# The opening stage of a hybrid encoder layer: staging of weights, form of the first norm, queue of its stores, and place of two projection tiles

## Chip, core and metric

One core of one Trainium2 chip. The metric is the time of one execution on the device in microseconds; of several runs the median counts. A profiled execution has a time of its own, which is given beside its span.

## What is computed

One encoder layer over 1024 prompt tokens and 64 sample tokens of width 1024. The change touches the first norm, the keys and values of the memory tokens, and the input projection:

```python
hp = _layer_norm(x_prompt, ln_in_g, ln_in_b)        # 1024 tokens
hs = _layer_norm(x_sample, ln_in_g, ln_in_b)        # 64 tokens
mk_p = (mem_prompt @ mem_w_k[l])                    # 256 x 1024, outputs mem_k_p
mv_p = (mem_prompt @ mem_w_v[l])                    # outputs mem_v_p
...
proj = x @ p['w_in']
g_q, g_k, g_v, g_o, g_a, s_u, f_q, f_k, f_v, f_f = jnp.split(proj, offsets, axis=-1)
o_gla, gla_s = _gla_mix(g_q, g_k, g_v, g_o, g_a, ...)
o_s5, s5_re, s5_im = _s5_mix(s_u, ...)

def _layer_norm(x, g, b):
    mu = jnp.mean(xf, axis=-1, keepdims=True)
    var = jnp.mean(jnp.square(xf - mu), axis=-1, keepdims=True)
    y = (xf - mu) * lax.rsqrt(var + LN_EPS) * g + b
```

Behind that come gated linear attention, the S5 state space model, forgetting attention, cross attention into the memory, and a gated ConvFFN. All of it is float32.

## The kernel before

Every matmul is made of three: each operand is split into a high part (`_hi`, `xh`, a rounded float32 that TensorE takes at full rate) and the remainder (`_lo`, `xl`), and `mm3` sums hi x hi, hi x lo and lo x hi. `split_weights` does it for a weight unit of 128 x 1024: SP (SyncE) starts the load into `raw`, ScalarE copies it to `hi`, and GpSimd or VectorE subtracts for `lo`. `raw` has two buffers, `hi` and `lo` have four.

The opening stage loads the memory tokens (`load_mem`, into the buffers of token tiles 6 and 7), transposes them (`mem_features`), and runs four halves of the memory projection (`mem_half`, two for keys and two for values, each over four weight units and two row tiles, out `ps_kv`). Nine token tiles `xr[i]` are loaded (`load_x`; five lie in `xra`, four in `xrb`), and `layer_norm` works on each: VectorE takes statistics (`bn_stats`), GpSimd computes the reciprocal deviation (`rstd_of`, `ln_y`) and the offset `ln_nb`, ScalarE scales in place, VectorE multiplies by `lnw[0]`, GpSimd adds `lnw[1]`. The tile is then stored to `hd` in DRAM from ScalarE's queue and transposed by `to_features` (TensorE into `ps_tr`, ScalarE copies `x0h`, VectorE subtracts `x0l`). Results of `mem_half` go through one buffer, `spare`, and ScalarE's queue to `out_mem_k` and `out_mem_v`. A one-column copy on GpSimd in `load_x` holds a tile's load back until a given weight unit has been split.

Next is the feature projection: `a_tiles` computes tiles of 128 features over all tokens (`ps_a`, two halves of 544 tokens, 96 matmuls of 272 columns for each tile). Tiles 0 and 1 are the S5 input; they are stored to DRAM as `suD` and read back in another layout as U by eight loads. Tiles 2 and 3 are the queries and keys of the linear attention (`gq`, `gk`). `b_proj` computes token-major parts (`ps_b`). The S5 stage runs in four quarters: VectorE computes parameters in a region called `s5r` (R3), GpSimd makes tables from them, TensorE reads U in `s_in` and gives `s_y`. Its parameters come into `p1s`, which lies where `lnw` was.

The program is written in one order, and a scheduler sets each engine's own order from it when the kernel is built, with priorities in the order of writing. At run time each engine and each queue takes its instructions strictly in that order, and a waiting instruction holds back those behind it.

Of the kernel before, what the change touches and what calls it, by code (L numbers as in the profile page):

```python
# [9 lines left out]
F32 = mybir.dt.float32  # L10
# [52 lines left out]
def hybrid_layer(ctx: ExitStack, tc: tile.TileContext, I, O):  # L63
# [45 lines left out]
    G.memset(mhalf, -0.5)  # L109


    def split_weights(src, n, name, eng=None):
        raw = mem.tile([128, 1024], F32, tag="raw", name=name + "_raw", bufs=2)
        hi = mem.tile([128, 1024], F32R, tag="whi", name=name + "_hi", bufs=4)
        lo = mem.tile([128, 1024], F32R, tag="wlo", name=name + "_lo", bufs=4)
        SY.dma_start(out=raw[:, :n], in_=src)
        S.activation(out=hi[:, :n], in_=raw[:, :n], func=AF.Copy)  # L117
        (eng or G).tensor_tensor(out=lo[:, :n], in0=raw[:, :n], in1=hi[:, :n].bitcast(F32), op=SUB)  # L118
        return hi, lo
# [145 lines left out]


    memT = [slot([128, 4, 256], F32R, "memT") for _ in range(4)]
    memx = xr[7], xr[6]
    mem_out = [O[n].rearrange("a b m h d -> (a b m) (h d)") for n in ("mem_k_p", "mem_v_p")]
    wm = []  # L270
    V.memset(xr[8], 0.0)
# [4 lines left out]
    def mem_units(n):  # L276
        for _ in range(n):
            j, u = divmod(len(wm), 4)
            wm.append(split_weights(I[("w_mk", "w_mv")[j // 2]][j % 2, :, 1024 * u:1024 * u + 1024], 1024, "wm",
                                    (V, V, G)[len(wm) % 3]))  # L280

    def mem_features(i):
        both = psd("ps_tr")
# [8 lines left out]
    def mem_half(j):  # L292
        pss = [pse("ps_kv") if j % 2 else pst("ps_kv") for _ in range(2)]
        for k in range(KD):
            w = [u.rearrange("p (k c) -> p k c", k=2)[:, k % 2, :] for u in wm[4 * j + k // 2]]
            for i in range(2):
                mm3(pss[i], [memT[2 * z + k // 4][:, k % 4, 128 * i:128 * i + 128] for z in range(2)], w, k == 0, k == KD - 1)
        for i in range(2):
            S.activation(out=spare, in_=pss[i], func=AF.Copy)
            S.dma_start(out=mem_out[j // 2][128 * i:128 * i + 128, 512 * (j % 2):512 * (j % 2) + 512], in_=spare)  # L300

    def load_x(i, after=None):
        t0, m = token_tile(i)
        if after is not None:
            G.tensor_copy(out=xr[i][:, 0:1], in_=after[0][:, 0:1].bitcast(F32))
        SY.dma_start(out=xr[i][0:m], in_=I["x_prompt"][0, t0:t0 + m, :] if i < 8 else I["x_sample"][0])

    load_mem(0)
    mem_units(2)
    load_mem(1)  # L310
    load_x(0)
    lnw = load_ln(I["ln_in_g"], I["ln_in_b"])
    load_x(1)
    mem_features(0)
    mem_features(1)
    mem_units(2)
    for i, u in zip(range(2, NT), (1, 3, 4, 5, 6, 8, 8)):
        load_x(i, wm[u])
        mem_units(min(2, 16 - len(wm)))
        if i % 2 == 0 and i < 8:  # L320
            mem_half(i // 2 - 1)
    mem_half(3)
    for i in range(NT):
        t0, m = token_tile(i)
        layer_norm(xr[i], lnw)
        S.dma_start(out=hd[128 * i:128 * i + 128, :], in_=xr[i])
        to_features(xr[i], xh, xl, t0, m, True)

    xst = slot([128, KD, 2, 64], F32R, "xst")
    for z in range(2):  # L330
# [357 lines left out]
    go = g5(NT, 256)  # L688
    V.memset(gv[64:128, 8, :], 0.0)
    V.memset(go[64:128, 8, :], 0.0)  # L690
    a_tile(2, plain_evac(gq))
    a_tile(3, plain_evac(gk))
    b_proj(b_weights("w_b1", 280, 3), 280, 3, b1_evac)
    a_tile(4, q_evac(0))
    b_proj(b_weights("w_b2", 256, 4), 256, 4, b2_evac)
# [1006 lines left out]
```

## Time and profile before

| | |
|---|---|
| median of 3 runs | 1766.38 us (1760.13 to 1768.58) |
| time of the profiled execution | 1761.28 us |
| its span, first to last instruction | 1759.6 us |
| TensorE busy in the span | 1658.4 us (94%) |
| mean granted clock of TensorE | 0.976 |

Busy is the time in which an engine had an instruction running. Matmuls overlap, so TensorE's busy time says when it stands still, and the interval between two starts says what a matmul takes. The granted clock is the share of full speed that TensorE was given; 0.5 is the lower of its two levels, 1.2 of 2.4 GHz. A wait is put down to what released the instruction last.

### The profile page before, as it was taken

How to read it: one execution, taken by the hardware profiler on the slowest of the kernel's cores; microseconds unless marked ns; L12 is line 12 of the kernel's file. 1: busy time of each engine (PE TensorE's matmuls, PEld its weight loads, DVE VectorE, ACT ScalarE, POOL GpSimd, SP SyncE). 2: the span in 40 equal slices, each digit the busy share in tenths (PEclk: the TensorE clock that was granted, in tenths of full speed). 3: DMA queues.
4: the chain of work that ended last, by engine and by line, in shares of the span. 5: the costliest groups of instructions: out<-in, count | busy, mean ns of one | idle time of the engine just before them, and what ended most of it. 6: DMA issues, size and time to landing. Idle time of an engine off the chain costs nothing.

```text
span 1759.6 us, 27862 instructions
## 1 busy us (share of the span) xinstructions
PE 1658.4 (94%) x10856; PEld 1457.0 (83%) x10856; DVE 1053.2 (60%) x1802; ACT 694.3 (39%) x1265; POOL 724.9 (41%) x774
## 2 busy tenths in 40 slices
PE   7788999999999999999999899999999999999997
PEld 5588987777767878988777789999999997777775
DVE  6673611665556336124444899877788786785547
ACT  4421224423655235235335654444444445221111
POOL 5765831111001256223223465554555447743322
PEclk9899999999989999999999899999999999999999
DMA  8633232436960410122111212222222227531112
GB/s 287 236 97 59 67 102 75 167 113 183 285 146 25 156 48 24 37 73 72 37 48 68 79 63 76 86 77 81 80 77 75 80 87 259 179 104 44 48 49 101
DMA packets 95754, 178.29 MB, mean 101 GB/s; under 512 B 26207, under 2 KB 48575, under 8 KB 95495
## 3 DMA queue, kind: packets, MB, share of 16 engines
q1 hardware_dynamic: 65462, 136.00, 25.6%
q10 hardware_dynamic: 30160, 40.52, 6.3%
q8 instruction: 85, 1.39, 0.3%
q14 instruction: 47, 0.38, 0.1%
HBM read 129.56 MB, written 46.34 MB: 100 GB/s over the span
## 4 chain that ended last, share of the span: by engine, by line
PE 43%; DVE 7%; issue 4%; POOL 3%; ACT 2%; DMA 2%; POOLq 0%; DVEq 0%; SPq 0%; ACTq 0%
PE ps_d L197 7%; PE u_a L1390 6%; PE u_d L1390 6%; PE u_c L1390 6%; PE ps_a L215 5%; PE ps_o L197 4%; PE u_b L1390 3%; PE m_o L197 1%; PE m_s L197 1%; POOL wd_lo L118 1%; DVE Yb L1556 1%; POOL ln_y L124 1%; DVE Ya L1556 1%; DMA hraw<-hD 1%; POOL ln_y L123 0%
## 5 line engine op out<-in xcount | busy, mean ns | idle before, releaser
L197 PE MATMUL ps_d<-wd_hi,hb 128*128 128x512 f32 x704 | 225.0, 396 | 10.7 <-DVE Ya L1556 3.0
L197 PEld LDWEIGHTS ps_d<-wd_hi,hb 128*128 128x128 f32 x704 | 132.1, 188 | 48.0 <-DVE Yb L1556 3.9
L197 PE MATMUL ps_d<-wd_lo,hb 128*128 128x512 f32 x352 | 139.6, 397 | 1.6 <-POOL wd_lo L118 1.6
L1390 PE MATMUL u_a<-x2A,wu_wlo 128*128 128x288 f32 (+1 forms) x1032 | 139.3, 291 | 0.9 <-DVE x2A L1201 0.9
L1390 PEld LDWEIGHTS u_a<-x2A,wu_wlo 128*128 128x128 f32 x1032 | 134.2, 192 | 1.3 <-DVE x2A L1201 1.3
L1336 POOL TENSOR_TENSOR wu_wlo<-wu_raw,wu_wlo 128x512 fp32r<-128x512 f32 x63 | 97.3, 1547 | 80.7 <-ACT wu_wlo L1335 80.7
L197 PE MATMUL ps_o<-wo_hi,bo 128*128 128x512 f32 x384 | 124.8, 399 | 3.0 <-ACT ps_o L138 2.7
L1463 DVE SCALAR_TENSOR_TENSOR y<-x2B,ffp,y 128x1024 f32<-128x1024 f32 x88 | 124.8, 1419 | 1.1 <-ACT y L1461 1.0
L1493 POOL TENSOR_TENSOR hb<-hraw,hb 128x1024 fp32r<-128x1024 f32 (+1 forms) x40 | 64.9, 1642 | 84.3 <-ACT hb L1492 84.3
L1336 POOL TENSOR_TENSOR wu_whi<-wu_whi 128x512 fp32r<-128x512 f32 x44 | 71.1, 1615 | 61.1 <-ACT wu_whi L1335 60.4
L197 PE MATMUL ps_b<-wb_hi,x0h 128*128 128x512 f32 (+2 forms) x256 | 89.6, 351 | 0.0
L197 PE MATMUL ps_b<-wb_lo,x0h 128*128 128x512 f32 (+2 forms) x256 | 89.2, 348 | 0.0
L197 PE MATMUL ps_b<-wb_hi,x0l 128*128 128x512 f32 (+2 forms) x256 | 89.0, 348 | 0.0
L1335 ACT ACTIVATE wu_wlo<-wu_raw 128x512 fp32r<-128x512 f32 x86 | 54.1, 631 | 88.4 <-DVE wu_raw L1332 34.7
L197 PEld LDWEIGHTS ps_o<-wo_hi,bo 128*128 128x128 f32 x384 | 72.6, 191 | 18.9 <-ACT ps_o L138 3.1
L1556 DVE TENSOR_TENSOR Ya<-Ya,ps_d 128x1024 f32<-128x1024 f32 (+1 forms) x50 | 60.9, 1218 | 44.8 <-PE ps_d L197 39.3
L1018 POOL TENSOR_TENSOR bo<-mixT,bo 128x512 fp32r<-128x512 f32 (+1 forms) x18 | 22.7, 1270 | 150.2 <-ACT bo L1017 150.2
L118 POOL TENSOR_TENSOR wo_lo<-wo_raw,wo_hi 128x1024 fp32r<-128x1024 f32 x14 | 33.2, 2383 | 118.6 <-ACT fx_pt L976 45.6
L197 PEld LDWEIGHTS ps_d<-wd_lo,hb 128*128 128x128 f32 x352 | 66.1, 188 | 17.1 <-POOL wd_lo L118 2.5
L197 PE MATMUL ps_o<-wo_lo,bo 128*128 128x512 f32 x192 | 76.6, 399 | 1.2 <-POOL wo_lo L118 1.2
L118 POOL TENSOR_TENSOR wa_lo<-wa_raw,wa_hi 128x1024 fp32r<-128x1024 f32 x16 | 38.9, 2445 | 93.0 <-ACT wa_hi L117 55.2
L1492 ACT ACTIVATE hb<-hraw 128x1024 fp32r<-128x1024 f32 (+1 forms) x40 | 25.3, 652 | 128.1 <-PE ps_d L197 115.8
(548 smaller groups left out, 4502.0 us busy)
## 6 DMA issues: line engine op xcount, KB each, us to landing
wu_raw<-in_w_up SPq DMA_DIRECT2D x88, 256.0 KB, 2.7
hD<-y ACTq DMA_DIRECT2D x22, 512.0 KB, 2.6
wd_raw<-in_w_dn SPq DMA_DIRECT2D x22, 512.0 KB, 3.5
hraw<-hD SPq DMA_DIRECT2D x20, 544.0 KB, 4.5
fx<-qk SPq DMA_DIRECT2D x28, 256.0 KB, 8.7
fxk<-qk SPq DMA_DIRECT2D x20, 256.0 KB, 4.8
wm_raw<-in_w_mk SPq DMA_DIRECT2D x8, 512.0 KB, 5.8
wm_raw<-in_w_mv SPq DMA_DIRECT2D x8, 512.0 KB, 5.4
```

Source lines behind the costliest of these rows:

```text
L118: (eng or G).tensor_tensor(out=lo[:, :n], in0=raw[:, :n], in1=hi[:, :n].bitcast(F32), op=SUB)
L124: G.tensor_tensor(out=y, in0=y, in1=mhalf[0:v.shape[0], 0:n], op=ALU.pow)
L197: PE.matmul(out, lhsT=lhs[i], rhs=rhs[j], start=start and n == 0, stop=stop and n == 2)
L215: PE.matmul(ps[:, c, 0:272], lhsT=w[i][:, k, :], rhs=xs[j][:, k, t0:t0 + 272], start=k == 0 and n == 0, stop=k == KD - 1 and n == 2)
L1018: G.tensor_tensor(out=sl, in0=part, in1=sh.bitcast(F32), op=SUB)
L1335: S.activation(out=WU[n][0], in_=RAW[n], func=AF.Copy)
L1336: (eng or G).tensor_tensor(out=WU[n][1], in0=RAW[n], in1=WU[n][0].bitcast(F32), op=SUB)
L1390: PE.matmul(ps, lhsT=w[i][:, k, :], rhs=x[j][:, k, c], start=start and k == 0 and q == 0, stop=k == 3 and q == 2, skip_group_check=True)
L1463: V.scalar_tensor_tensor(out=out, in0=u[:, c + j:c + j + n], scalar=cw[j][:, m:m + 1], in1=out, op0=MUL, op1=ADD)
L1492: S.activation(out=t[:, hi:hi + n], in_=r, func=AF.Copy)
L1493: G.tensor_tensor(out=t[:, lo:lo + n], in0=r, in1=t[:, hi:hi + n].bitcast(F32), op=SUB)
L1556: V.tensor_tensor(out=x, in0=x, in1=p, op=ADD)
```

## The change

Five edits:

- The memory tokens and all weight units of the memory projection but the first two are loaded into `stage`, a tile over the region R3 that is not in use yet, in six places by turns, so that they don't share the two `raw` buffers. The memory tokens lie in places 6 and 7 of it, and one of two output buffers (`outs`) behind them. VectorE subtracts three units of four, GpSimd the second of each four.
- `first_norm` replaces `layer_norm` here. The two last steps are two `scalar_tensor_tensor` operations on VectorE: (x - mu) * g, then * y + b. For tiles 0, 2 and 8 the statistics stay on VectorE; for the other six ScalarE makes the sum and the sum of squares by accumulation in two passes (the second writes into `xh`, which the transposes overwrite later).
- Stores of the memory projection and of `hd` are started by SP, in the queue of the loads.
- Loads and norms are written between the halves of the memory projection, and the copies on GpSimd that held loads back are gone.
- `a_tile(2)` and `a_tile(3)` are written around the loads of U instead of behind the S5 stage.

```diff
-    def split_weights(src, n, name, eng=None):
-        raw = mem.tile([128, 1024], F32, tag="raw", name=name + "_raw", bufs=2)
+    def split_weights(src, n, name, eng=None, raw=None):
+        if raw is None:
+            raw = mem.tile([128, 1024], F32, tag="raw", name=name + "_raw", bufs=2)
...
-    memx = xr[7], xr[6]
+    stage = region(R3, KD * EXT, F32, "stage")
+    memx = [stage[:, 1024 * j:1024 * j + 1024] for j in (6, 7)]
+    outs = spare, stage[:, 8192:8704]
...
+            n = (len(wm) - 2) % 6
             wm.append(split_weights(I[("w_mk", "w_mv")[j // 2]][j % 2, :, 1024 * u:1024 * u + 1024], 1024, "wm",
-                                    (V, V, G)[len(wm) % 3]))
+                                    G if len(wm) % 4 == 1 else V, stage[:, 1024 * n:1024 * n + 1024] if len(wm) > 1 else None))
...
-            S.activation(out=spare, in_=pss[i], func=AF.Copy)
-            S.dma_start(out=mem_out[j // 2][128 * i:128 * i + 128, 512 * (j % 2):512 * (j % 2) + 512], in_=spare)
+            S.activation(out=outs[i], in_=pss[i], func=AF.Copy)
+            SY.dma_start(out=mem_out[j // 2][128 * i:128 * i + 128, 512 * (j % 2):512 * (j % 2) + 512], in_=outs[i])
...
-        if after is not None:
-            G.tensor_copy(out=xr[i][:, 0:1], in_=after[0][:, 0:1].bitcast(F32))
...
+    def first_norm(i):
+        x, (t0, m) = xr[i], token_tile(i)
+        if i not in (0, 2, 8):
+            sm = small([128, 1], "ln_sums")
+            S.activation(out=x, in_=x, func=AF.Identity, accum_out=sm)
+            mv = small([128, 2], "ln_mv")
+            V.tensor_scalar(out=mv[:, 0:1], in0=sm, scalar1=-1.0 / 32768, scalar2=None, op0=MUL)
+            S.activation(out=xh[:, :, t0:t0 + 128], in_=x.rearrange("p (k c) -> p k c", k=KD), func=AF.Square, scale=1.0 / 32,
+                         bias=mv[:, 0:1], accum_out=mv[:, 1:2])
+            mu = small([128, 1], "ln_mu")
+            V.tensor_scalar(out=mu, in0=sm, scalar1=1.0 / 1024, scalar2=None, op0=MUL)
+        else:
+            mv = mean_var(x, None)
+            mu = mv[:, 0:1]
+        y = rstd_of(mv[:, 1:2], 1, "ln")
+        V.scalar_tensor_tensor(out=x, in0=x, scalar=mu, in1=lnw[0], op0=SUB, op1=MUL)
+        V.scalar_tensor_tensor(out=x, in0=x, scalar=y, in1=lnw[1], op0=MUL, op1=ADD)
+        to_features(x, xh, xl, t0, m, True)
...
+    for j in range(4):
+        load_x(2 * j + 2)
+        if j < 3:
+            mem_units(2)
+            load_x(2 * j + 3)
+        mem_half(j)
+        if j < 3:
+            mem_units(2)
+        first_norm(2 * j)
+        first_norm(2 * j + 1)
+    first_norm(8)
     for i in range(NT):
-        t0, m = token_tile(i)
-        layer_norm(xr[i], lnw)
-        S.dma_start(out=hd[128 * i:128 * i + 128, :], in_=xr[i])
-        to_features(xr[i], xh, xl, t0, m, True)
+        SY.dma_start(out=hd[128 * i:128 * i + 128, :], in_=xr[i])
...
     a_tiles(I["w_a"], xs, [(tt, su_evac(tt)) for tt in range(2)])
+    a_tile(2, plain_evac(gq))
     for j in range(8):
         SY.dma_start(out=U[16 * (7 - j):16 * (8 - j)], in_=suD.rearrange("(g c) j n -> c j g n", c=16)[:, j])
+    a_tile(3, plain_evac(gk))
...
-    a_tile(2, plain_evac(gq))
-    a_tile(3, plain_evac(gk))
```

Three places show how the instructions stand in a row. A number behind an x counts equal neighbours.

SP's queue in the second half of the opening stage. Before, from the load of token tile 4 on, it holds loads alone (`wm_raw` are weight units, `xra` and `xrb` token tiles):

```order
L306 DMA xra<-in_x_prompt 128x1024
L116 DMA wm_raw<-in_w_mk 128x1024 x2
L306 DMA xrb<-in_x_prompt 128x1024
L116 DMA wm_raw<-in_w_mv 128x1024
L306 DMA xrb<-in_x_prompt 128x1024
L116 DMA wm_raw<-in_w_mv 128x1024 x3
L306 DMA xrb<-in_x_prompt 128x1024
L306 DMA xrb<-in_x_sample 64x1024
L116 DMA wm_raw<-in_w_mv 128x1024 x4
```

After, all token tiles and the first two `wa` units are loaded before this place, and stores stand among the last eight weight units, which land in `stage`:

```order
L351 DMA hd<-xra 128x1024
L117 DMA stage<-in_w_mv 128x1024
L351 DMA hd<-xra 128x1024
L117 DMA stage<-in_w_mv 128x1024 x3
L304 DMA out_mem_k_p<-xrb 128x512
L304 DMA out_mem_k_p<-stage 128x512
L117 DMA stage<-in_w_mv 128x1024
L351 DMA hd<-xra 128x1024
L117 DMA stage<-in_w_mv 128x1024
L351 DMA hd<-xra 128x1024 x2
L351 DMA hd<-xrb 128x1024
L117 DMA stage<-in_w_mv 128x1024 x2
```

Six stores of `hd` and two of `out_mem_k` have moved in front of weight loads; each waits at its place until its tile is ready.

VectorE at the end of the stage. Before, the first operation of the S5 parameters (the first row here) stands in front of the last six of the `x0l`:

```order
L462 TENSOR_SCALAR s5r<-p1s 128x16
L455 TENSOR_SCALAR p1s<-p1s 128x2
L456 TENSOR_TENSOR s5r<-ident,p1s 16x256
L536 TENSOR_TENSOR s5r<-p1s 128x16
L463 TENSOR_SCALAR s5r<-s5r 128x16
L537 TENSOR_TENSOR s5r<-p1s 128x16
L191 TENSOR_TENSOR x0l<-ps_tr,x0h 128x4x128
```

After:

```order
L119 TENSOR_TENSOR wm_lo<-stage,wm_hi 128x1024 x2
L192 TENSOR_TENSOR x0l<-ps_tr,x0h 128x4x128 x2
L481 TENSOR_SCALAR p1s<-p1s 128x2
L192 TENSOR_TENSOR x0l<-ps_tr,x0h 128x4x128 x2
L482 TENSOR_TENSOR s5r<-ident,p1s 16x256
L488 TENSOR_SCALAR s5r<-p1s 128x16
L562 TENSOR_TENSOR s5r<-p1s 128x16
L563 TENSOR_TENSOR s5r<-p1s 128x16
L489 TENSOR_SCALAR s5r<-s5r 128x16
L564 TENSOR_TENSOR s5r<-s5r 128x16
L490 TENSOR_SCALAR s5r<-s5r 128x16
L192 TENSOR_TENSOR x0l<-ps_tr,x0h 128x4x128
```

Six `x0l` stand behind the first S5 operation (on `p1s`) still, and four of them behind the first that writes `s5r` (two are those of tile 8). But `s5r` lies in R3, where `stage` is now, so that its first write has to wait until the last load, read and store of `stage` are through.

TensorE in front of the first `s_in`. Before, it stands among the matmuls of tile 2 (`gq`):

```order
L215 MATMUL ps_a<-x0l,wa_hi 128x272 x2
L215 MATMUL ps_a<-x0h,wa_lo 128x272 x2
L215 MATMUL ps_a<-x0h,wa_hi 128x272
L629 MATMUL s_in<-g_698,s5r 128x137 x4
L215 MATMUL ps_a<-x0h,wa_hi 128x272
L215 MATMUL ps_a<-x0l,wa_hi 128x272 x2
```

After, tiles 2 and 3 are through, the first quarter's small products `ko_ps` and `ebt` too, and 29 matmuls of the first `b_proj` have run:

```order
L216 MATMUL ps_a<-x0h,wa_lo 128x272 x2
L632 MATMUL ko_ps<-s5r 16x128 x4
L641 MATMUL ebt<-ident,s5r 128x128 x4
L198 MATMUL ps_b<-wb_hi,x0h 128x280
L198 MATMUL ps_b<-wb_lo,x0h 128x280
...
L198 MATMUL ps_b<-wb_lo,x0h 128x280
L655 MATMUL s_in<-g_663,s5r 128x137 x4
L198 MATMUL ps_b<-wb_hi,x0l 128x280
```

Between the first `ps_a` and the first `s_in` there were 295 matmuls, and there are 425.

## Rows read from the trace of the kernel before

**Rows 1.** Windows: us; PE, PEld, DVE, ACT, POOL busy (instructions); clock; DMA; GB/s.

```profile
0.00:22.00 22.00, 11.94 (x46) 8.59 (x46) 12.43 (x22) 9.23 (x11) 8.80 (x23) 1.00 0.88 302
22.00:60.00 38.00, 31.70 (x128) 24.45 (x129) 24.99 (x34) 20.35 (x26) 28.65 (x29) 0.87 0.81 277
0.00:94.00 94.00, 67.20 (x277) 50.93 (x277) 60.83 (x97) 46.17 (x57) 61.01 (x64) 0.91 0.77 261
```

**Rows 2.** Timeline of PE: start, length, operation, count, idle before.

```profile
72.73 0.62 PE L197 MATMUL ps_kv<-wm_hi,memT 128*128 128x512 f32 x2
...
73.41 0.39 PE L197 MATMUL ps_kv<-wm_hi,memT 128*128 128x512 f32 x1
...
86.80 0.39 PE L197 MATMUL ps_kv<-wm_hi,memT 128*128 128x512 f32 x1
...
93.97 0.80 PE L215 MATMUL ps_a<-x0h,wa_hi 128*128 128x272 f32 x2
```

**Rows 3.** Waits of PE, 0 to 94 us: total, times, longest.

```profile
PE ps_kv L197 <- POOL wm_lo L118: 6.0, 3, 3.5
```

**Rows 4.** Groups of VectorE, 0 to 94 us: busy, mean ns, idle before.

```profile
L118 DVE TENSOR_TENSOR wm_lo<-wm_raw,wm_hi 128x1024 fp32r<-128x1024 f32 x11 | 16.2, 1487 | 9.3 <-ACT wm_hi L117 9.3
L191 DVE TENSOR_TENSOR x0l<-ps_tr,x0h 128x512 fp32r<-128x512 f32 x16 | 10.7, 675 | 2.4 <-ACT x0h L190 2.4
L142 DVE BATCH_NORM_STATS2 ln_st<-xra 128x6 f32<-128x512 f32 x10 | 6.4, 682 | 4.2 <-DMA xra<-in_x_prompt 4.2
L155 DVE TENSOR_TENSOR xra<-xra,lnw 128x1024 f32<-128x1024 f32 x5 | 6.3, 1256 | 1.3 <-ACT xra L151 1.3
L290 DVE TENSOR_TENSOR memT<-ps_tr,memT 128x512 fp32r<-128x512 f32 x4 | 2.7, 683 | 4.7 <-ACT memT L289 4.7
L143 DVE BATCH_NORM_AGGREGATE ln_mv<-ln_st 128x2 f32<-128x12 f32 x9 | 1.7, 196 | 0.1
```

**Rows 5.** Timeline of VectorE and GpSimd around 61.5 us.

```profile
61.52 3.42 DVE L155 TENSOR_TENSOR xrb<-xrb,lnw 128x1024 f32<-128x1024 f32 x1
...
61.45 2.40 POOL L156 TENSOR_TENSOR xrb<-xrb,lnw 128x1024 f32<-128x1024 f32 x1
```

**Rows 6.** Nearest operations elsewhere: line 1463 (min/median/max ns), and ScalarE's squaring pass.

```profile
L1463 DVE SCALAR_TENSOR_TENSOR y<-x2B,ffp,y x88: 1271/1277/2818, 1031.7 to 1473.8; 128x1024 f32<-128x1024 f32 x88
...
L166 ACT ACTIVATE ln_sq<-Yb,ln_mv 128x1024 f32<-128x1024 f32 x4 | 4.6, 1152 | 20.0 <-DVE ln_mu L167 11.1 <-DVE ln_mv L164 8.9
```

**Rows 7.** Groups of ScalarE and GpSimd in the norm, 0 to 94 us.

```profile
L151 ACT ACTIVATE xra<-xra,ln_nb,ln_y 128x1024 f32<-128x1024 f32 x5 | 6.1, 1238 | 2.9 <-POOL ln_nb L150 2.9
L156 POOL TENSOR_TENSOR xra<-xra,lnw 128x1024 f32<-128x1024 f32 x5 | 13.9, 2770 | 5.3 <-DVE xra L155 5.3
```

**Rows 8.** DMA issues, 0 to 130 us: count, KB each, median us to landing.

```profile
out_mem_v_p<-xrb ACTq DMA_DIRECT2D x4, 256.0 KB, 5.0
```

**Rows 9.** Timelines of PE, SP, GpSimd and VectorE around the first `s_in`.

```profile
134.45 0.41 PE L215 MATMUL ps_a<-x0h,wa_lo 128*128 128x272 f32 x2
134.70 0.29 PE L215 MATMUL ps_a<-x0h,wa_hi 128*128 128x272 f32 x1
140.54 2.17 PE L629 MATMUL s_in<-g,s5r 128*128 128x137 f32 x8 [5.55 <-DMA s5r<-s5r]
...
142.73 0.65 PE L215 MATMUL ps_a<-x0l,wa_hi 128*128 128x272 f32 x2
...
128.67 4.62 SPq L430 DMA_DIRECT2D g<-suD  x8
...
127.75 1.99 POOL L118 TENSOR_TENSOR wb_lo<-wb_raw,wb_hi 128x840 fp32r<-128x840 f32 x1
...
86.69 2.21 DVE L462 TENSOR_SCALAR s5r<-p1s 128x16 f32<-128x16 f32 x1 [3.14 <-DMA p1s<-in_s_par]
```

**Rows 10.** Window in the last S5 quarter, columns as in Rows 1.

```profile
228.00:236.00 8.00, 6.76 (x44) 6.76 (x45) 3.50 (x7) 0.39 (x1) 3.42 (x7) 0.79 0.00 0
```

More of the change, by code (lines that the diff above doesn't have):

```diff
@@ L298, in mem_half, with load_x @@
         for i in range(2):
-            S.activation(out=spare, in_=pss[i], func=AF.Copy)
-            S.dma_start(out=mem_out[j // 2][128 * i:128 * i + 128, 512 * (j % 2):512 * (j % 2) + 512], in_=spare)
-    def load_x(i, after=None):
+            S.activation(out=outs[i], in_=pss[i], func=AF.Copy)
+            SY.dma_start(out=mem_out[j // 2][128 * i:128 * i + 128, 512 * (j % 2):512 * (j % 2) + 512], in_=outs[i])
+    def load_x(i):
         t0, m = token_tile(i)
-        if after is not None:
-            G.tensor_copy(out=xr[i][:, 0:1], in_=after[0][:, 0:1].bitcast(F32))
         SY.dma_start(out=xr[i][0:m], in_=I["x_prompt"][0, t0:t0 + m, :] if i < 8 else I["x_sample"][0])
+    def first_norm(i):
[16 more added lines that the diff above has]
+        to_features(x, xh, xl, t0, m, True)
     load_mem(0)
-    mem_units(2)
+    mem_units(1)
+    load_x(0)
+    mem_units(1)
     load_mem(1)
-    load_x(0)
     lnw = load_ln(I["ln_in_g"], I["ln_in_b"])
@@ L316, in hybrid_layer @@
     mem_units(2)
[L317 to L322, printed above, removed]
+    for j in range(4):
[9 more added lines that the diff above has]
+    first_norm(8)
     for i in range(NT):
-        t0, m = token_tile(i)
-        layer_norm(xr[i], lnw)
-        S.dma_start(out=hd[128 * i:128 * i + 128, :], in_=xr[i])
-        to_features(xr[i], xh, xl, t0, m, True)
+        SY.dma_start(out=hd[128 * i:128 * i + 128, :], in_=xr[i])
     xst = slot([128, KD, 2, 64], F32R, "xst")
```

## The prediction

> **What bounds the kernel now.** I read the stretch before the first matmul of the feature projections by its windows first. TensorE starts `ps_a` at 93.97 us [rows 2]. Until then the memory projection has 192 matmuls of 512 columns, and three of them take 0.68 us where nothing waits [rows 2], so 192 x 0.227 = 43.6 us; with the transposes the 94 us hold little more than half their length in work. The rest is waiting and a granted clock of 0.91 on average [rows 1]; the longest wait in total is for the low halves of weights that GpSimd subtracts [rows 3]. No engine is full there: VectorE is busy 60.8 us of 94, GpSimd 61.0, ScalarE 46.2, the transfers 0.77 [rows 1]. Behind this stage TensorE is nearly always busy, so a microsecond taken out here arrives at the end, unless a later wait takes it. The next wait is at 134.7 us: TensorE stops 5.55 us before the first `s_in` matmul, which reads U, and then runs at half speed for a while (a pair of 272 columns takes 0.65 us at 142.7 and 0.41 at 134.45) [rows 9].
>
> **Opening stage, engine by engine, after the change.**
>
> GpSimd loses the nine additions of the norm's offset (five of them 13.9 us) [rows 7], nine `ln_nb`, seven copies that held back x loads and one of five weight subtractions. It stops being what TensorE waits for.
>
> ScalarE loses nine scaling passes of 1.24 us and the issue of 17 stores, and gets two passes for each of six tiles, one of 1.24 [rows 7] and one like the squaring pass of 1.15 [rows 6]: 14.3 for 11.1 us. Of 94 us it was busy 46, so this is covered as long as weights arrive no faster than they do now.
>
> VectorE: up to the low half of the last weight unit it has 12 subtractions at 1.49 (17.8 us), 6 statistics at 0.68 (4.1), 18 of the new two-tensor operations, 10 `x0l` at 0.68 (6.8), 4 `memT` at 0.68 (2.7), and some 15 small ones at up to 0.2 (3) [rows 4]. The new operation isn't in this stage; the same form in the ConvFFN takes 1.271 us at least, 1.277 in the median, 2.82 at most [rows 6]. I take 1.277 because GpSimd has only six large operations left here: 23.0 us. Sum 57.4 us. It starts at some 6.5 us, as now, and early on waits about 3 us for loads: 67 us.
>
> Transfers: the bytes stay. What changes is the order in SP's queue: 23 loads in a row (11.8 MB), then the eight w_mv units with six `hd` stores and two `out_mem_k` stores among them (7.9 MB). So the last weight unit lands after 19.7 MB. At 302 GB/s, the rate of the first 22 us, in which nearly all are loads [rows 1], that is 65.2 us, and some 2.8 us until the first has landed: 68. At 277 GB/s, the rate of 22 to 60 us [rows 1], it is 74. If a busy share of 0.88 at 302 GB/s could be full, 343 GB/s and 60 us. I take 302, since the stage begins with loads alone and no buffer holds them back. One high half (1.06 us, ScalarE) and one low half (1.23 on VectorE) behind it: 70.3. So transfers end some 3 us behind VectorE, two things that end close together.
>
> TensorE then has 10 of the last unit's matmuls, 2.3 us: the projection ends at 72.6, where it ends at 87.2 now. From there to the first `ps_a` it is 6.8 us now [rows 2]. That part gets longer. VectorE's queue has the first write into `s5r` in front of two of the last `x0l`, and `s5r` lies where weights were staged, so that write waits for the last `out_mem_v` store out of that region: two copies and two issues 2.2 us, landing 5.0 [rows 8], then small operations and two `x0l`, 2.3 us: 9.5 us. First `ps_a` at 82 us, **12 us earlier**. With the ends for transfers: 88 us at 277 GB/s, and 79 where VectorE's 67 decides; 6 to 15 us.
>
> **The two feature tiles.** They add nothing: 192 matmuls stand earlier, in front of `s_in`. Now 295 matmuls lie between the first `ps_a` and `s_in`, then 425, of 0.125 us (0.25 a pair [rows 9]) to 0.135: 54 us, and 3.3 us for the slow clock and the wait for tile 8 at the start, which are there now as well. TensorE reaches `s_in` at about 139 us. U: its chain begins with VectorE's first S5 operation, now at 86.69 us, and SP starts the U loads at 128.67, 42 us later [rows 9]. In the new queue they stand behind a `wa` load that waits for GpSimd's second `wb` subtraction, which ends at 129.74 now, 43 us behind the chain's start [rows 9]. The chain now starts when the store has landed, 72.6 + 7.2 = 80 us; U loads at 123.5, the eight issued in 4.6 us and landed in some 7 more: 135. TensorE comes at 139 and doesn't stop. Of the 5.55 us and the 2.3 lost to half speed behind them (4.7 us at half) **7.5 us** are gained; if U came 4 us later than this, still all but one; 4 to 8.
>
> From there on GpSimd's tables set the pace of the four S5 quarters. The matmuls between the `s_in` groups are as many as now or more (183, 192 and 227; now 183, 184 and 193), so what hides the tables stays. Now TensorE loses 1.24 us of waiting and 1.7 of clock at the last quarter [rows 10]. I put the difference at 0, with -4 to +2 us.
>
> The stores of `hd` are needed far later; their cover is the whole S5 stage. The memory stores on SP free ScalarE from waiting in a line with them.
>
> **Sum.** The profiled run took 1761.3 us: 1761.3 - 12 - 7.5 = 1741.8. It lies 5.1 us under the median of the runs shown, which spread over 8.5 us; I put the new median at **1744**.
>
> One rule is weighed against these rows. In the trace a VectorE product that began just after a GpSimd sum of 2.40 us took 3.42 us [rows 5], where the mean of its like on the other buffer is 1.26 [rows 4]: it lost what GpSimd had left to run. By the mean rows such meetings are few, which gives the 1744 above; with one for each of the six large GpSimd operations left, the sum is that of the first rival. The Trainium skill (SBUF — State Buffer, "Who interferes with whom") makes this case a rule: a VectorE operation with two SBUF inputs shares a read port with GpSimd, the port is a lock, and the later of the two is blocked outright; each of the new operations can be blocked so.
>
> **Rivals.**
>
> *VectorE is blocked or the transfers run at the lower rate.* Each collision costs 3.42 - 1.26 = 2.2 us; six in a row add 13 us to 67, `ps_a` then at 92, and the gain is the tiles' 7.5 alone: 1754. The lower rate gives 88, total 1748. For it: VectorE and transfers end within 3 us of each other, in a chain where each new norm feeds a store that stands in front of a weight load in the same queue. Against it: stores wait for norms that end 10 us and more before their turn. 1748 to 1757, chance 0.18.
>
> *The S5 chain eats it.* If the chain begins 4 us later or a table takes longer than its 24 us of matmuls, TensorE waits at each `s_in`, as it does now at the first and the last; the opening's gain shrinks to what the chain itself moved (6.7 us) less one more stall. 1757 to 1768, no change: 0.11. That the change does nothing in the opening is part of it; the fill in rows 1 speaks against.
>
> *Slower: the staging region.* `s5r` now can't be touched before the last `out_mem_v` store has landed, and in SP's queue this store stands behind two `wa` loads, each of which waits for a GpSimd subtraction and that for a free weight buffer on TensorE. Each link is 2 to 5 us. If they add up in line instead of running beside the projection, the chain starts at 72.6 + 30 rather than + 7, U lands at 158, and TensorE stops 19 us at `s_in`: 1761.3 - 12 + 19 = 1768 in the profiled time. It decides from a chain start of some 100 us on, 13 us later than now. I give it 0.07: the two `wa` tiles need units 12 and 13 only, which are through some 5 us before the last.
>
> *More.* Transfers at 343 GB/s, no collision, `ps_a` at 76 to 79, and the last quarter's loss gone: 1726 to 1736. 0.10.
>
> **Chances.** Forecast (1736 to 1750) 0.54, the two limited rivals 0.18 and 0.11, more 0.10, slower 0.07. A change under 0.5%, about 9 us, can't be told from none here. Faster: 0.54 + 0.10 + 0.16 = 0.80; same 0.13; slower 0.07. From 1730 to 1759 the cases left out are the best part of "more" and the "no change" above 1759 with the slower one, under 2 in 10.
>
> **What the new profile would show.** Right: the first `ps_a` between 79 and 88 us; the last `ps_kv` at 70 to 77; `s_in` without a wait of more than 2 us, at 135 to 142; `scalar_tensor_tensor` on `xra` and `xrb` near 1.28 us; SP waiting for no norm longer than a microsecond or two. Wrong: TensorE waiting for `wm_lo` on VectorE for more than 8 us in all; new operations above 2 us; VectorE's first `s5r` operation later than 90 us; a wait at `s_in` as long as now; or the time coming back in the later quarters as waits for GpSimd's tables.

## The result and the profile after

| | before | after |
|---|---|---|
| median, 4 runs each | 1764.79 us | 1746.10 us (1743.71 to 1751.33) |
| profiled execution | 1761.28 us, span 1759.6 | 1746.15 us, span 1744.4 |
| last `ps_kv` ends | 87.2 us | 75.8 us |
| first `ps_a` | 93.97 us | 84.29 us |
| last `ps_b` of `wb_hi` and `x0h` starts | 360.7 us | 345.5 us |

The ratio is 0.9894, 95% interval 0.9876 to 0.9912, so 18.7 us are gone (15.5 to 21.9); 19.5 were forecast. One execution each of two kernels below, the tiles alone and the stores on SP alone, took far longer (3216 and 2292 us), and their ratios leave it out. The change moves every line number: loads are L117 now, high halves L118, low halves L119, `x0l` L192, `mm3` L198, `ps_a` L216, `s_in` L655, the two new operations L325 and L326, the `hd` store L351.

The windows of the kernel after, with columns as in [rows 1], which the first, second and last row answer:

```profile
0.00:22.00 22.00, 14.38 (x60) 10.73 (x61) 14.16 (x24) 11.18 (x15) 7.65 (x17) 1.00 0.93 348
22.00:60.00 38.00, 29.55 (x128) 22.58 (x127) 37.73 (x46) 26.37 (x42) 18.45 (x17) 0.87 1.00 355
40.00:46.00 6.00, 2.36 (x10) 1.35 (x10) 6.00 (x12) 5.57 (x10) 4.31 (x6) 0.91 1.01 406
46.00:52.00 6.00, 2.74 (x7) 2.16 (x8) 6.00 (x5) 3.31 (x5) 2.44 (x2) 0.50 1.03 419
0.00:94.00 94.00, 72.84 (x336) 58.40 (x337) 72.77 (x152) 51.93 (x78) 38.03 (x40) 0.89 0.76 270
```

GpSimd fell from 61.0 to 38.0 us busy, and VectorE has hardly a gap left between 22 and 60 us (37.73 of 38). The transfers are busy nearly all the time there, and move more than 400 GB/s between 40 and 52 us, where only large ones are started. TensorE stands still for more than half of these 12 us, and its granted clock falls to 0.50, the lower level.

The timeline shows this place, the end of the stage, and `s_in`. Columns as in [rows 2]; ACT is ScalarE, SPq the queue that SP starts transfers from:

```profile
17.70 1.23 DVE L119 TENSOR_TENSOR wm_lo<-stage,wm_hi 128x1024 fp32r<-128x1024 f32 x1 [0.74 <-ACT wm_hi L118]
...
28.66 2.03 SPq L1237 DMA_DIRECT2D g<-in_ln_b  x1
31.23 4.00 SPq L351 DMA_DIRECT2D hd<-xra  x1
35.33 0.38 SPq L117 DMA_DIRECT2D stage<-in_w_mv  x1
...
41.77 1.05 ACT L118 ACTIVATE wm_hi<-stage 128x1024 fp32r<-128x1024 f32 x1
...
45.52 2.60 POOL L119 TENSOR_TENSOR wm_lo<-stage,wm_hi 128x1024 fp32r<-128x1024 f32 x1 [0.49 <-ACT wm_hi L118]
...
45.96 3.25 DVE L119 TENSOR_TENSOR wm_lo<-stage,wm_hi 128x1024 fp32r<-128x1024 f32 x1
...
49.26 0.80 PE L198 MATMUL ps_kv<-wm_lo,memT 128*128 128x512 f32 x1 [3.45 <-DVE wm_lo L119]
...
75.44 0.39 PE L198 MATMUL ps_kv<-wm_hi,memT 128*128 128x512 f32 x1
...
83.51 1.11 PE L189 MATMUL ps_tr<-ident,xrb 128*128 128x128 f32 x4 [3.07 <-DVE x0l L192]
84.29 0.82 PE L216 MATMUL ps_a<-x0h,wa_hi 128*128 128x272 f32 x2
...
118.50 4.80 SPq L455 DMA_DIRECT2D g<-suD  x8
...
140.62 0.29 PE L198 MATMUL ps_b<-wb_lo,x0h 128*128 128x280 f32 x1
140.75 1.10 PE L655 MATMUL s_in<-g,s5r 128*128 128x137 f32 x8
```

The first w_mv unit (the ninth of sixteen) is started by SP at 35.33 us, behind small loads and a store in its queue. ScalarE copies it at 41.77, and VectorE subtracts it only at 45.96, behind norm operations. TensorE has done the 96 matmuls of w_mk and two that need the high half alone, and waits for that low half until 49.26. From there to 75.8 it runs 94 matmuls and 16 transposes without a gap. `s_in`, which started at 140.54 behind 5.55 us of waiting in [rows 9], now starts at 140.75 right behind another matmul, with no wait.

TensorE's waits, first from 0 to 94 us as in [rows 3], then from 142 to 300 us, and last the one line of the kernel before in that stretch:

```profile
PE ps_tr L189 <- DVE x0l L192: 5.7, 3, 3.1
PE ps_kv L198 <- DVE wm_lo L119: 5.2, 4, 3.5
PE ps_kv L198 <- ACT wm_hi L118: 2.9, 1, 2.9
PE ps_kv L198 <- POOL wm_lo L119: 1.0, 1, 1.0
...
PE s_y L673 <- DVE s5r L663: 1.9, 1, 1.9
PE glu L703 <- DMA g<-zD: 1.1, 1, 1.1
PE ps_b L198 <- ACT fv_st L264: 1.0, 1, 1.0
PE ga_x L775 <- ACT p1s L751: 0.9, 1, 0.9
PE fg_t L748 <- ACT p1s L751: 0.9, 1, 0.9
```

```profile
PE s_in L629 <- DVE s5r L630: 2.9, 2, 2.3
```

GpSimd's 6.0 us of low halves became 1.0, and VectorE's took their place. In the S5 stage and behind it, the 2.9 us at later `s_in` are gone, and small waits have come elsewhere that were not there.

VectorE's groups from 0 to 94 us, as in [rows 4]; the new operations answer the row of line 1463 in [rows 6]:

```profile
L119 DVE TENSOR_TENSOR wm_lo<-stage,wm_hi 128x1024 fp32r<-128x1024 f32 x11 | 17.5, 1594 | 3.0 <-ACT wm_hi L118 3.0
L326 DVE SCALAR_TENSOR_TENSOR xra<-xra,ln_y,lnw 128x1024 f32<-128x1024 f32 x5 | 6.4, 1278 | 0.4 <-POOL ln_y L125 0.4
L326 DVE SCALAR_TENSOR_TENSOR xrb<-xrb,ln_y,lnw 128x1024 f32<-128x1024 f32 x4 | 5.1, 1270 | 0.0
```

### The profile page after: what moved, and what is told of

Read it like the earlier page. It is cut to its first block, busy times and chain, and to the rows that moved or that the text cites. A ratio compares the mean times of both kernels' runs of the same rounds, so it can differ in the third digit from the quotient of the medians.

```text
span 1744.4 us, 27851 instructions
## 1 busy us (share of the span) xinstructions
PE 1651.9 (95%) x10856; PEld 1451.6 (83%) x10856; DVE 1057.6 (61%) x1806; ACT 695.3 (40%) x1280; POOL 698.9 (40%) x748
## 4 chain that ended last, share of the span: by engine, by line
PE 44%; DVE 8%; issue 4%; POOL 2%; ACT 2%; DMA 2%; POOLq 0%; SPq 0%; DVEq 0%; ACTq 0%
PE u_a L1414 7%; PE ps_d L198 7%; PE u_d L1414 6%; PE u_c L1414 6%; PE ps_a L216 6%; PE ps_o L198 5%; PE u_b L1414 3%; PE m_o L198 1%; POOL wd_lo L119 1%; PE m_s L198 1%; DVE Yb L1580 1%; DVE y L1487 1%; DVE Ya L1580 1%; DMA hraw<-hD 1%; DMA kv_p<-out_mem_v_p 1%
## 5 line engine op out<-in xcount | busy, mean ns | idle before, releaser
L198 PE MATMUL ps_d<-wd_hi,hb 128*128 128x512 f32 x704 | 225.1, 396 | 11.3 <-DVE Ya L1580 3.5
L198 PEld LDWEIGHTS ps_d<-wd_hi,hb 128*128 128x128 f32 x704 | 132.1, 188 | 47.9 <-DVE Yb L1580 3.9
L198 PE MATMUL ps_d<-wd_lo,hb 128*128 128x512 f32 x352 | 139.0, 395 | 1.3 <-POOL wd_lo L119 1.3
L198 PE MATMUL ps_o<-wo_hi,bo 128*128 128x512 f32 x384 | 126.5, 403 | 3.0 <-ACT ps_o L139 2.7
L198 PE MATMUL ps_b<-wb_hi,x0h 128*128 128x512 f32 (+2 forms) x256 | 89.5, 350 | 1.0 <-ACT fv_st L264 1.0
L198 PEld LDWEIGHTS ps_o<-wo_hi,bo 128*128 128x128 f32 x384 | 72.7, 191 | 20.0 <-ACT ps_o L139 3.1
L198 PE MATMUL ps_b<-wb_lo,x0h 128*128 128x512 f32 (+2 forms) x256 | 88.4, 346 | 0.4 <-POOL wb_lo L119 0.4
L198 PE MATMUL ps_b<-wb_hi,x0l 128*128 128x512 f32 (+2 forms) x256 | 88.6, 346 | 0.0
L119 POOL TENSOR_TENSOR wo_lo<-wo_raw,wo_hi 128x1024 fp32r<-128x1024 f32 x14 | 33.2, 2383 | 118.5 <-ACT fx_pt L1000 45.6
L198 PEld LDWEIGHTS ps_d<-wd_lo,hb 128*128 128x128 f32 x352 | 66.1, 188 | 16.9 <-POOL wd_lo L119 2.2
L119 POOL TENSOR_TENSOR wa_lo<-wa_raw,wa_hi 128x1024 fp32r<-128x1024 f32 x16 | 39.2, 2454 | 101.0 <-ACT wa_hi L118 67.8
L198 PE MATMUL ps_o<-wo_lo,bo 128*128 128x512 f32 x192 | 77.1, 402 | 1.1 <-POOL wo_lo L119 1.1
```

The costliest lines, as they stand in the source:

```text
L198: PE.matmul(out, lhsT=lhs[i], rhs=rhs[j], start=start and n == 0, stop=stop and n == 2)
```

## Experiments

Each was timed beside the kernel before on the same chip; ratios are to it. Theory A of the first experiments is one: the opening is set by VectorE and by what collides with it, and the two tiles cover the stop at `s_in` independently.

**The tiles alone.** Kernel before, with

```diff
+    a_tile(2, plain_evac(gq))
     for j in range(8):
         SY.dma_start(out=U[16 * (7 - j):16 * (8 - j)], ...
+    a_tile(3, plain_evac(gk))
...
-    a_tile(2, plain_evac(gq))
-    a_tile(3, plain_evac(gk))
```

> The kernel before, with nothing changed but the place of tiles 2 and 3 (written around the loads of U). Theory A: the stop of 5.55 us at the first s_in and the 2.3 us of half speed behind it are all that the two tiles cover, and nothing takes it back. First ps_a stays at 94, s_in comes at 150 to 153 without a wait above 1 us, and the time falls by 5 to 8 us: 1757 to 1760 (ratio 0.995 to 0.997). Theory B: GpSimd's tables pace the S5 quarters, so the stop only moves to a later quarter; the time stays within 2 us of the kernel before, and TensorE waits more than 4 us in all at later s_in or s_y.

Measured: 1752.81 us, ratio 0.9940 (0.9927 to 0.9952), 10.3 us less, where A had 8 at most. The profile is that of another execution of the same kernel:

> The kernel before with nothing changed but the place of tiles 2 and 3, looked at again for its profile (that of the first run was taken in a disturbed execution). It took 10.3 us off, where the stop at s_in and the half speed behind it are 7.9. Theory A: the stop is gone, and the 2 to 3 us more come from the later quarters, where the waits of 2.9 us at s_in are gone too. Theory B: the opening itself is shorter, first ps_a before 92 us.

1752.27 us. Its timeline at `s_in`:

```profile
151.79 0.30 PE L197 MATMUL ps_b<-wb_lo,x0h 128*128 128x280 f32 x1
151.92 1.10 PE L631 MATMUL s_in<-g,s5r 128*128 128x137 f32 x8
```

and TensorE's waits from 142 to 320 us:

```profile
PE s_y L649 <- DVE s5r L639: 1.9, 1, 1.9
PE glu L679 <- DMA g<-zD: 1.1, 1, 1.1
PE ps_b L197 <- ACT fv_st L263: 1.0, 1, 1.0
```

The first `ps_a` stands at 94.6, so the second B, a shorter opening, is out; and with 10.3 us gained the first one is too. The stop is gone, as A says, but the small waits of the kernel after come with the tiles: they are not the opening's doing, and the later quarters give nothing more. The last `ps_b` starts 5.7 us earlier than before. The span is 9.8 us shorter; the other 4.1 us arise bit by bit behind that `ps_b`, where this edit touches nothing. TensorE lost 3.9 us less there to the granted clock (1 minus clock, added up over windows of 4 us: 23.3 us against 27.2). The kernel after has the same tiles and gains nothing in this stretch (1398.9 us, as before), so these 4 us are not shown to be the tiles' doing.

**The opening alone.** The changed kernel with `a_tile(2)` and `a_tile(3)` back behind the S5 code (the diff above, reversed).

> The changed kernel with tiles 2 and 3 put back behind the S5 code; the new opening alone. Theory A: the opening gives its 9.7 us (first ps_a at 84 to 85), and since the S5 chain begins 7.4 us earlier too, the stop at s_in stays as long as in the kernel before or 2 us longer: 5.5 to 8 us of waiting, time 1753 to 1757 (ratio 0.993 to 0.995 to the kernel before). Theory B: without the tiles the S5 chain eats the opening's gain: the stop at s_in is 13 us or more, and the time is 1760 to 1765.

1749.90 us, ratio 0.9922 (0.9910 to 0.9935): 13.2 us. The first `ps_a` is at 83.5, and the stop at `s_in` is as long as before:

```profile
128.32 2.16 PE L653 MATMUL s_in<-g,s5r 128*128 128x137 f32 x8 [5.23 <-DMA s5r<-s5r]
```

A's mechanism holds: the S5 chain moved with the opening. Its numbers were a little off: `ps_a`, the stop and the time lie each just below its ranges.

**Stores in ScalarE's queue.** The changed kernel with

```diff
-            SY.dma_start(out=mem_out[...], in_=outs[i])
+            S.dma_start(out=mem_out[...], in_=outs[i])
...
-        SY.dma_start(out=hd[128 * i:128 * i + 128, :], in_=xr[i])
+        S.dma_start(out=hd[128 * i:128 * i + 128, :], in_=xr[i])
```

> The changed kernel with the stores of this stage (hd and the memory outputs) started by ScalarE again. Theory A: the queue of the stores is worth little, since ScalarE is busy 52 of 94 us: within 2 us of the changed kernel, 1744 to 1748, first ps_a within 2 us of 84.3. Theory B: a store that waits for its norm in ScalarE's queue holds up the high halves of weights behind it, which are what TensorE waits for; first ps_a at 88 or later and 1750 or more.

1761.89 us, ratio 0.9991 (0.9978 to 1.0004): 17.5 of the 18.7 us are lost; the first `ps_a` stands at 97.4. ScalarE's timeline:

```profile
16.48 0.19 ACT L314 ACTIVATION_READ_ACCUMULATOR xra<-xra 128x1 f32 x1
30.85 0.35 ACTq L351 DMA_DIRECT2D hd<-xra  x1
31.25 1.06 ACT L118 ACTIVATE wm_hi<-stage 128x1024 fp32r<-128x1024 f32 x1 [14.58 <-DMA xrb<-in_x_prompt]
```

A is out; B is right in the size and wrong in the reason. The tile to be stored had long been ready: its norm ended at 15.7 us. The program gives its transfers eight semaphores in turn, and a transfer waits until the one with the same semaphore has landed. Three rows of the order with what each waits for (`DMAHW` is such a semaphore), the first of SP's queue, the others of ScalarE's:

```
L308 DMA xrb<-in_x_prompt 128x1024 [waits DMAHW3_49]
...
L351 DMA hd<-xra 128x1024 [waits DMAHW3_49,DVE_49]
L118 ACTIVATE wm_hi<-stage 128x1024 [waits DMAHW0_49]
```

The store of the first tile waits for the load of a late one, and the copy that makes a high half stands behind it. In SP's queue nothing but later transfers stands behind such a wait. The Trainium skill (DMA: Bandwidth & Descriptors, "Issuing engines are not separate DMA queues") says that starting transfers from several engines saves only the time of starting them. By that page's sentence, and as an estimate, 17 starts of some 0.35 us or 6 us in all would be at stake here. The measurement decides: what an engine waits for ahead of a start stops it too, 14.6 us in one place.

**The norm in its old form.** The changed kernel with `layer_norm` in place of the sums and the two operations:

```diff
     def first_norm(i):
         x, (t0, m) = xr[i], token_tile(i)
...
-        V.scalar_tensor_tensor(out=x, in0=x, scalar=mu, in1=lnw[0], op0=SUB, op1=MUL)
-        V.scalar_tensor_tensor(out=x, in0=x, scalar=y, in1=lnw[1], op0=MUL, op1=ADD)
+        layer_norm(x, lnw)
         to_features(x, xh, xl, t0, m, True)
```

> The changed kernel with the norm in its old form (statistics on VectorE for all nine tiles, scaling on ScalarE, product on VectorE, sum on GpSimd); staging, order, queue and tiles stay changed. Theory A: the form is what frees GpSimd, and with the nine sums of 2.4 us and more back, collisions with VectorE come back too: first ps_a at 89 to 94, time 1751 to 1757. Theory B: VectorE is what is full in the changed opening (37.7 us of 38 between 22 and 60), and the old form has 9 operations of 1.26 us less there for 12 statistics of 0.68 us more, so it costs nothing: first ps_a at 82 to 86, time 1744 to 1748.

1751.66 us, ratio 0.9928 (0.9910 to 0.9946): 7.3 us are lost; the first `ps_a` at 89.2. VectorE's groups from 0 to 94 us:

```profile
L119 DVE TENSOR_TENSOR wm_lo<-stage,wm_hi 128x1024 fp32r<-128x1024 f32 x11 | 24.0, 2199 | 0.0
...
L156 DVE TENSOR_TENSOR xrb<-xrb,lnw 128x1024 f32<-128x1024 f32 x4 | 8.4, 2120 | 1.2 <-ACT xrb L152 1.2
```

A is right: with GpSimd's nine sums back, a subtraction takes 2.20 us on the mean where the changed kernel has 1.59 and an undisturbed one takes 1.21.

**Weights through two buffers.** The changed kernel with

```diff
-                                    G if len(wm) % 4 == 1 else V, stage[:, 1024 * n:1024 * n + 1024] if len(wm) > 1 else None))
+                                    G if len(wm) % 4 == 1 else V, None))
```

> The changed kernel with the weights of the memory projection loaded through the two raw buffers again; the memory tokens and one output buffer stay in stage, all else stays changed. Theory A: in the changed kernel up to eight transfers are under way and move 410 GB/s, and with two buffers each load waits for a subtraction on VectorE or GpSimd, and the stores behind it in SP's queue wait too; first ps_a at 88 to 94, time 1750 to 1757. Theory B: VectorE's fill sets the end of the stage, whatever the transfers do; first ps_a within 2 us of 84.3, time 1744 to 1749.

1744.35 us, ratio 0.9890 (0.9870 to 0.9910): leaving the staging of weights out costs nothing that can be seen. The projection ends 11 us later, but the transposes have filled its gaps, and `ps_a` follows at once, at full speed (a pair starts 0.25 us behind the last, in the changed kernel 0.45 for the first 4.5 us):

```profile
84.67 0.50 PE L198 MATMUL ps_kv<-wm_lo,memT 128*128 128x512 f32 x1 [0.53 <-DVE wm_lo L119]
...
87.10 0.41 PE L216 MATMUL ps_a<-x0h,wa_hi 128*128 128x272 f32 x2
87.35 0.41 PE L216 MATMUL ps_a<-x0l,wa_hi 128*128 128x272 f32 x2
```

Neither theory has this: transfers run slower (254 GB/s between 22 and 60 us), and VectorE isn't full (33.8 of 38 us), and the time is the same.

**Eight places in stage:**

```diff
-            n = (len(wm) - 2) % 6
+            n = (len(wm) - 2) % 8
```

> The changed kernel with eight places in stage instead of six (the two of the memory tokens are used again for units 8 and 9), so that the first two w_mv units needn't wait for a place. Theory A: TensorE starves between 40 and 53 us because these two units come late; they come 2 to 4 us earlier, TensorE's idle time there shrinks from 7 to under 5 us, first ps_a at 80 to 83, time 1741 to 1745 where the changed kernel has 1746. Theory B: it starves because norm operations stand in front of the low halves on VectorE, which is full; time within 1.5 us of the changed kernel.

1741.33 us, ratio 0.9865 (0.9843 to 0.9888). VectorE subtracts the first w_mv unit at 34.64 instead of 45.96 us; TensorE is busy 9.5 of 12 us between 40 and 52 instead of 5.1:

```profile
71.12 0.40 PE L198 MATMUL ps_kv<-wm_hi,memT 128*128 128x512 f32 x1
...
77.70 0.60 PE L216 MATMUL ps_a<-x0h,wa_hi 128*128 128x272 f32 x1 [1.26 <-DVE x0l L192]
```

The projection ends 4.3 us earlier, and `ps_a` starts 6.6 us earlier, further than A had it. The profiled execution is the fastest of the five, 1733.4 us, so these marks may flatter the edit, and the intervals of the two ratios overlap. That an earlier first unit moves the end of the projection is borne out; that it had waited for a place is not: in the changed kernel VectorE's first subtraction out of `stage` frees it at 18.93 us, and SP starts the load at 35.33, when its turn in the queue comes. With eight places the scheduler puts this load in front of those of `xrb`, and SP starts it at 16.89 us. So the run shows the worth of an earlier load, and the order in the queue made it early.

**Norms written in front of the last half.**

```diff
-        mem_half(j)
         if j < 3:
+            mem_half(j)
             mem_units(2)
...
     first_norm(8)
+    mem_half(3)
```

> The changed kernel with the norms of tiles 6, 7 and 8 written in front of the last half of the memory projection. The scheduler leaves the norms where they are, but puts two of the last four x0l and their transposes in front of the S5 operations. Theory A: the 8.5 us between the last ps_kv and the first ps_a shrink by 2 to 4, and the time follows: 1742 to 1744.5. Theory B: the S5 chain begins later by as much, and TensorE waits at s_in or in the quarters instead: 1745 to 1748.

1740.06 us, ratio 0.9860 (0.9844 to 0.9876). The first `ps_a` comes at 83.3, only 1.0 us earlier; from the end of `ps_kv` it is 6.7 us instead of 8.5. So A's mechanism is there a little under its range (1.8 us of 2 to 4), and most of the 5 us gained on the changed kernel came from elsewhere, unexplained.

**Stores on SP alone.** The kernel before with the queue's edit only.

> The kernel before, with nothing changed but that SP starts the stores of hd and of the memory outputs. Theory A: the queue decides only where many loads are under way, since a store waits until the transfer eight places ahead of it has landed, and here two raw buffers keep few loads under way; so alone it is worth little: first ps_a within 3 us of 94, time within 3 us of the kernel before (ratio 0.998 to 1.002). Theory B: the 16 us that the changed kernel loses with ScalarE's queue are the queue's own worth, and it gives most of the opening's gain by itself: first ps_a at 84 to 88, ratio under 0.996.

1759.15 us, ratio 0.9969 (0.9956 to 0.9983), between the two theories. The first `ps_a` is 2.9 us earlier, as A has it, and this is lost again at `s_in`, whose stop grows from 5.55 us by nearly as much:

```profile
139.16 2.17 PE L629 MATMUL s_in<-g,s5r 128*128 128x137 f32 x8 [8.37 <-DMA s5r<-s5r]
```

At the last `ps_b` it has gained 0.2 us. The trace gains 2.0 us more behind it, the medians differ by 4.9; no term of the edit accounts for either.

**Two buffers, and stores in ScalarE's queue.** The diffs of the third and the fifth experiment together.

> The changed kernel with weights through the two raw buffers and with the stores in ScalarE's queue: the new order and the new norm are left, and the tiles. Theory A: without staging fewer loads are under way, so ScalarE's longest stop in front of a high half shrinks from 14.6 us to under 6, and the loss against the changed kernel from 16 us to under 8: time 1746 to 1754 (ratio 0.990 to 0.995). Theory B: the store waits for loads in any case, since token tiles and the first weights are loaded ahead without raw buffers: a stop of 12 us or more, ratio 0.997 to 1.001.

1750.96 us, ratio 0.9928 (0.9912 to 0.9944). ScalarE's waits from 0 to 94 us have this in place of the 14.6:

```profile
ACT x0h L317 <- DMA xrb<-in_x_prompt: 5.9, 1, 5.9
```

A is right: the queue is worth 6.2 us without staging and 17.5 with it. Staging makes ScalarE's queue dear for the stores; that it does so by having more loads under way fits the shorter stop.

**More work on VectorE.** The changed kernel with

```diff
         V.scalar_tensor_tensor(out=x, in0=x, scalar=y, in1=lnw[1], op0=MUL, op1=ADD)
+        if i not in (0, 2, 8):
+            more = small([128, 2, 6], "ln_more")
+            for c in range(2):
+                V.bn_stats(out=more[:, c, :], in_=x[:, 512 * c:512 * c + 512])
```

> The changed kernel with two more statistics operations of 0.68 us on VectorE for each of six tiles, which nobody reads: 8.2 us more of VectorE's time in the opening, nothing else. Theory A: VectorE is full from 22 to 60 us and sets the end of the stage: first ps_a at 90 to 93, time 6 to 9 us over the changed kernel (1752 to 1755, ratio 0.993 to 0.996). Theory B: it is transfers or the order of the weights that set it, VectorE's queue only happens to be packed: first ps_a within 3 us of 84.3, ratio within 0.002 of the changed kernel's 0.9894.

1741.30 us, ratio 0.9872 (0.9853 to 0.9891), if anything faster than the changed kernel. The window 22 to 60 us, columns as in [rows 1]:

```profile
22.00:60.00 38.00, 28.20 (x120) 21.24 (x120) 38.00 (x51) 26.24 (x41) 18.98 (x17) 0.87 0.96 345
```

and the last `ps_kv` in the timeline:

```profile
76.04 0.40 PE L198 MATMUL ps_kv<-wm_hi,memT 128*128 128x512 f32 x1
```

A is out, and with it the theory that I had held so far. VectorE was given 7.6 us more, and the projection ends 0.6 us later (76.4 instead of 75.8). The load isn't the only difference: the scheduler put a norm operation behind the first w_mv subtraction, and the collision with GpSimd fell on a norm operation (3.12 us at 45.62) instead of that subtraction. TensorE goes on with that unit 1.3 us later, at 50.59; what VectorE does behind it no longer reaches the end.

Work that nobody reads came out as fast as the eight places (1741.33) and nearly as the norms in front (1740.06). So the times can't tell these versions from the changed kernel; what those two runs show they show by the marks in their traces, and not by their medians.

**The norm alone.** The kernel before with `first_norm` in place of `layer_norm` at its old place.

> The kernel before, with nothing changed but the form of the first norm (sums on ScalarE for six tiles, two operations of two tensors on VectorE, no sum on GpSimd), at the old place. Theory A: GpSimd's low halves are what TensorE waits for most in the kernel before, and nine sums of 2.4 us and more stand in front of them; without these the form alone gives 4 to 8 us: first ps_a at 86 to 90, ratio 0.9955 to 0.998. Theory B: GpSimd still holds the x loads back by its copies and loads are paced by two raw buffers, so the form alone gives under 2 us.

1761.32 us, ratio 0.9985 (0.9972 to 0.9997), 2.7 us (0.5 to 4.9). The last `ps_kv` comes 6.1 us later than before and the first `ps_a` 0.9 earlier, at 93.1, so A is out. B fits: the form frees GpSimd (37.6 us busy instead of 61.0), and the loads are still paced by two buffers and by the copies that hold them back; that these are the reason is argued, not shown.

| edit | alone | left out of the change |
|---|---|---|
| tiles moved | -10.3 us | +5.5 |
| stores on SP | -4.9 | +17.5 |
| form of the norm | -2.7 | +7.3 |
| staging of weights | not run | -0.6 |
| order of loads and norms, no holding copies | not run | not run |

Differences of medians, to the kernel before on the same chip; the right column is -18.7 set against each run's own gain. The values aren't sums of each other: the queue and the form of the norm pay more when the rest of the change is there. For the queue the pair of runs with and without staging shows why; for the norm no run does. The order of loads and norms was never taken alone or left out, so its share of the opening's 13.2 us is open. With the form and the tiles, but with two buffers and ScalarE's queue, it makes 13.1 us (the run with both diffs above), and tiles and form alone add up to 13.0.

## Why the prediction came out right

**The sum.** 1744 was forecast, 1746.1 measured. Both terms were somewhat too large, and each for a reason that the prediction did not have. In the two traces they make up 15.2 us (9.7 and 5.5), which is the whole difference of the spans: from the last `ps_b` to the end both take 1398.9 us. The terms of the forecast came to 19.5 us, and the medians differ by 18.7. So the total agrees better than its parts do, and that is luck: executions of one kernel scatter by 7 us and more.

**The opening, -12 us; measured -9.7** (84.29 against 93.97). *VectorE's sum* was good: it had been busy 56.05 us when its last low half ended at 66.60, where the prediction had 57.4 and 67. That the end itself was met to half a microsecond is luck. VectorE's last two subtractions wait 0.72 and 1.57 us for high halves, and ScalarE's copies wait for TensorE to give one of the four buffers free:

```profile
ACT wm_hi L118 <- PE ps_kv L198: 7.6, 3, 4.6
```

```profile
65.37 1.23 DVE L119 TENSOR_TENSOR wm_lo<-stage,wm_hi 128x1024 fp32r<-128x1024 f32 x1 [1.57 <-ACT wm_hi L118]
```

By then TensorE paced VectorE, and not the other way round. *The transfers' 68 us* was wrong: they ran at nearly full share and at up to 419 GB/s, above the bound of 343 that scaled the share up to one. The last weight load was started by 50.2 us and had landed before 60. *"TensorE then has 10 of the last unit's matmuls, 2.3 us"* is the step that failed. When VectorE was through, TensorE still had 36 matmuls to start, and the projection ended at 75.8 instead of 72.6. It had starved at 40 to 49 us, for the first unit of w_mv, and ran at the lower clock for some microseconds behind that; from 49.2 it was itself what set the end. The unread statistics (0.6 us at the end for 7.6 us on VectorE) and the eight places (4.3 us from an earlier unit) bear it out from both sides. A sum over the whole stage says when an engine is through, not whether its products come when they are wanted.

*The 9.5 us to the first `ps_a`* were 8.5. The wait is where I had it, at the last `x0l` (3.07 us), but the store out of `stage` had little part in it. It landed just in time: SP's load into `s5r`, which waits for it, starts at 79.20, and VectorE's first write into `s5r` follows the `x0l` in front of it at once, at 79.33. What stands in the way is 3.4 us of small S5 operations, 2.3 of them in one.

**The tiles and `s_in`, -7.5 us; measured -5.5 net.** TensorE arrives at 140.75 (139 was forecast) and doesn't wait, the loads of U start at 118.5 (123.5). The term for the later quarters was taken as 0 with -4 to +2: it is about +2, and the small waits that the moved tiles bring are of that size (6.5 us between 142 and 320 us, against 3.4 in the kernel before); the run with the tiles alone has the same ones. Less is left to run beside the S5 chain: 130 matmuls more are done before the first `s_in`, and I had compared the matmuls between the `s_in` groups and not those behind the last. That this is the cause is argued, not shown.

**VectorE blocked.** Two collisions of this kind happened before 66 us, not six, and with subtractions (3.34 and 3.25 us), not with the new operations (1.27 us in most, 1.65 at most). The second lies on the path: 3.25 us instead of 1.21, ending 1.09 us behind GpSimd's own. That VectorE gets through only when GpSimd is done agrees with the Trainium skill (SBUF — State Buffer, "Who interferes with whom"). The old norm shows what more of them cost.

**The S5 chain eats it.** Not here; but the stores on SP alone lost their 2.9 us in just this way.

**The staging region.** The chain starts at 79.3 us, where 80 was forecast and 100 would have been too late. SP waited 5.3 us for norms on `xrb`, 2.7 at most, more than the microsecond or two that was forecast, but behind the last weight load; the 4 us at its first `hd` store were not a norm's, which was through at 15.8.

**What had no price.** The prediction gives the queue of the stores one sentence ("free ScalarE from waiting in a line with them"). It is worth 17.5 us in this kernel. The wait ahead of a start was not read, though the semaphores of the transfers stand in the order of the changed kernel.

## What to carry to other kernels

When a stage is fed by a stream of units, look for the longest gap between two of them at the consumer, and at the place of the late unit in its queue; engine sums and fill come after that. Let transfers that may wait be started by an engine that no other work stands behind, above all when loads are let run ahead. Price an edit both alone and by leaving it out: here the largest by the one is not the largest by the other.

## What the runs showed of the hardware

Windows of 6 us in which the transfers' busy share was about one (0.97 to 1.06) moved 300 to 371 GB/s in the opening of the kernel before and 287 to 419 in that of the kernel after, 406 to 419 from 40 to 52 us with large transfers alone; so the share can't be scaled up to a rate. Small loads among the large ones are a likely reason for the low values, not tested.

Starts behind a load of 1024 single elements took long: in the kernel after 2.03 us for the second such load and 4.00 us for the `hd` store behind it, in the kernel before 2.69 us for the second load and 2.79 for the weight load behind it, where a start takes 0.3 to 0.6.

Between kernels, the stretch from the last `ps_b` to the end, which no edit touches, took 1394.4 to 1399.9 us in ten of the traces. What TensorE lost there to the granted clock, added up as above, lies between 21.5 and 27.2 us (1394.4 with 21.5 for the eight places, 1394.8 with 23.3 for the tiles alone, 1398.9 with 27.2 before), and its idle time between 61.8 and 66.3. The two together follow the length of the stretch, so what differs is how the single execution ran there; why the clock differs is open.
